# A chunked recurrence: the inverse's rows paced by the state's update, its operand fetched earlier, and half of the last norm's factors on ScalarE

## The chip, the cores and the metric

The kernel runs on one core of one Trainium2 chip. The metric is device time in microseconds (us), from the first to the last instruction with what lies around them; three runs stand behind the time before. The engines are TensorE (PE; PEld are its weight loads), VectorE (DVE), ScalarE (ACT), GpSimd (POOL) and SyncE (SP), whose queue issues nearly all DMAs.

## What is computed

A trunk of two layers on x of 2048 x 1024: first sliding-window attention, then RWKV-7 time mixing, each with a gated branch from per-layer inputs. The change touches the second layer's recurrence and the last RMS norm:

```python
def step(S, inp):                      # one token, 16 heads of 64 x 64 state
    sa = einsum('bhvk,bhk->bhv', S, -kk_t)
    S = S * d_t + sa[..., None] * (kk_t * a_t) + v_t[..., None] * k_t
    y = einsum('bhvk,bhk->bhv', S, r_t)
    return S, y
...
h = h + m
h = h + jax.nn.sigmoid(h @ ple_w_gate[i]) * (p[i] @ ple_w_proj[i])
return rms_norm(h, final_norm_g)
```

## The kernel before

Four phases follow each other: the attention's projections, the attention, the recurrence's projections and, from about 1950 us on, the recurrence (`rwkv`, L1176 on). The kernel computes the recurrence in 32 chunks of 64 tokens. Within a chunk the dependence of tokens on each other is a triangular system, whose inverse is needed for each of 16 heads; between chunks the state S is carried.

**Steps.** All work is written as Python generators, and `tick` (L574) advances each of the live ones by one `yield`. One tick is a step. `Dense.run` (L143) writes one step's worth of a dense product in each: three matmuls of 128x512 (L587 to L589, high and low parts of the operands), with the fetches, splits and evacuations around them. The recurrence's `chain(c)` (L1353) writes the chunk itself and puts steps between its parts: r1p (L1359) and 4 steps; y, up (L1371, L1379) and 5 steps; sp (L1386), the state's update and 9 steps. The update is st = sp + S on VectorE (L1388), two products uv = st x decay for the two halves (L1391), and S = st x decay on GpSimd (L1392). The next chunk's r1p reads uv. So a chunk has 18 steps, and a group of four chunks 72; in the text below, steps of a group are counted from 0, and its last chunk begins at step 54. Ahead of its steps a chunk writes its loads: `uv_tile(c + 1)`, bvt and szt (`load_bz`, L1405), x and xa of chunk c + 2 (`load_front`, L1229 to L1236). The former chunk's output is scaled in step 4 of a chunk and stored (gated, L1450).

**The inverse.** `tri(g)` (L1272) makes the inverses of four chunks at once, during the four chunks before them; `tris` (L1334) starts it when the first of these begins. Its operand ag (one buffer) comes by `load_ab` (L1340). Four transpositions (L1280), one per step, bring ag into P; GpSimd masks P (L1282); after three empty steps 30 rows follow, each a product into tmp (L1291) and a sum into P (L1293), of up to 240 elements per partition:

```python
for r in range(30, 0, -1):
    ...
    for _ in range(2 if r % 2 and 6 < r < 26 else 1):
        yield
```

Then come eight transpositions into at and tt (L1301, L1304), a copy on ScalarE (L1307), and twice, for two chunks each, products with ag (L1316), copies, four empty steps, products with tt (L1323) and copies. After the second half and one more step, `load_ab(g + 1)` is written. Counted so, the rows stand in steps 7 to 46 of a group, the second half's L1316 in step 61, its L1323 in step 65, and the load in step 66.

**The last norm.** `add_gate1` (L401) takes one of four column blocks n of 512 tokens: after its last tile, rs is made (L435 to L437, the power on GpSimd), and in eight further steps each of eight tiles res of 128x512 is multiplied by it (L442: k = 1 and 5 on GpSimd, the other six on VectorE) and stored (L443).

**Order.** The program is built with `schedule_with_timeline_sim=True` (L1503): the framework builds each engine's queue itself from the instructions as written and their dependences. Each queue then runs in its order on the chip, and an instruction at its head that has to wait holds those behind it.

Of the kernel before, what the change touches and what calls it, by code (L numbers as in the profile page):

```python
# [11 lines left out]
AF = mybir.ActivationFunctionType  # L12
ALU = mybir.AluOpType
# [7 lines left out]
NG = T // G  # L21
# [31 lines left out]
class Dense:  # L53
# [347 lines left out]
    def add_gate1(self, kind):  # L401

        tr, nc, ins = self.tr, self.nc, self.tr.ins
        NB = G // 128
        own, hs, sums = [], {}, {}

        def evac(n, ct, ps, hl, aux):
            th = self.tmp("th")
            self.gated(th, ps, hl, aux, (n, ct) == (NG - 1, KT - 1))
            if not own:  # L410
                own.append(self.cp.tile([128, C], F32, name="gnb"))
                nc.sync.dma_start(out=own[0], in_=ins["final_norm_g"].rearrange("(o c) -> o c", o=1).broadcast_to([128, C]))
            if ct == 0:
                sums[n] = self.cp.tile([128, NB, KT], F32, name="ss", bufs=2)
            ss = sums[n]
            for _ in range(9):
                yield
            for b in range(NB):
                nc.tensor.transpose(ps[:, b * 128:b * 128 + 128], th[:, b * 128:b * 128 + 128], tr.ident)
            res = hs[ct] = self.tmp("res", tag="h")  # L420
            blocks = lambda t: t.rearrange("p (b c) -> p b c", c=128)
            g = own[0][:, ct * 128:ct * 128 + 128].rearrange("p (o c) -> p o c", o=1).broadcast_to([128, NB, 128])
            last = (n, ct) == (NG - 1, KT - 1)
            if not last:
                nc.vector.tensor_tensor(out=blocks(res), in0=blocks(ps), in1=g, op=ALU.mult)
            for b in range(NB):
                sl = slice(b * 128, b * 128 + 128)
                nc.scalar.activation(th[:, sl], ps[:, sl], AF.Square, accum_out=ss[:, b, ct:ct + 1])
            if last:
                nc.vector.tensor_tensor(out=blocks(res), in0=blocks(ps), in1=g, op=ALU.mult)  # L430
            if ct < KT - 1:
                return
            yield
            rs = self.cp.tile([128, NB], F32, name="rs", bufs=2)
            nc.vector.tensor_reduce(out=rs, in_=ss, axis=mybir.AxisListType.X, op=ALU.add)  # L435
            nc.vector.tensor_scalar(out=rs, in0=rs, scalar1=1.0 / C, scalar2=1e-6, op0=ALU.mult, op1=ALU.add)
            nc.gpsimd.tensor_tensor(out=rs, in0=rs, in1=tr.mhalf.broadcast_to([128, NB]), op=ALU.pow)  # L437
            f = rs.rearrange("p (b o) -> p b o", o=1).broadcast_to([128, NB, 128])
            for k in range(KT):
                yield  # L440
                e = nc.gpsimd if k % 4 == 1 else nc.vector
                e.tensor_tensor(out=blocks(hs[k]), in0=blocks(hs[k]), in1=f, op=ALU.mult)  # L442
                nc.sync.dma_start(out=tr.out[n * G:n * G + G, k * 128:k * 128 + 128].rearrange("(b p) c -> p b c", p=128),  # L443
                                  in_=blocks(hs[k]))

        self.add(kind, w=ins["ple_w_gate"][1], fill=self.fill_direct, aux=self.load(tr.dram("ple1", [C, T])),
                 evac=evac, after="o")


class Trunk:  # L450
# [725 lines left out]
    def rwkv(self):  # L1176
        nc, ins = self.nc, self.ins
        LC = 64
        NP = KT
        NCH = T // LC  # L1180
        TG = 4
# [4 lines left out]
        with ExitStack() as es:  # L1186
# [85 lines left out]
            def tri(g):  # L1272


                ag = AG.pop(g)
                P = sm.tile([128, 32, 32], F32, name="P")
                PT = P.rearrange("u s t -> u t s")
                ga = ag.rearrange("q p c t -> q t (p c)")
                for i in range(0, 32, 8):
                    nc.vector.transpose(PT[:, i:i + 8], ga[:, i:i + 8])  # L1280
                    yield
                nc.gpsimd.affine_select(out=P, in_=P, pattern=[[-1, 32], [1, 32]], compare_op=ALU.is_gt, fill=0.0, base=0,  # L1282
                                        channel_multiplier=0)
                nc.gpsimd.memset(P.rearrange("u s t -> u (s t)")[:, 0:1024:33], 1.0)
                tmp = sm.tile([128, 240], F32, name="tmp")
                for _ in range(3):
                    yield
                for r in range(30, 0, -1):
                    n = 31 - r
                    t = tmp[:, 0:r * n].rearrange("u (s t) -> u s t", t=n)  # L1290
                    nc.vector.tensor_tensor(out=t, in0=P[:, 0:r, r:r + 1].broadcast_to([128, r, n]),  # L1291
                                            in1=P[:, r:r + 1, r + 1:].broadcast_to([128, r, n]), op=ALU.mult)
                    nc.vector.tensor_tensor(out=P[:, 0:r, r + 1:], in0=P[:, 0:r, r + 1:], in1=t, op=ALU.add)  # L1293
                    for _ in range(2 if r % 2 and 6 < r < 26 else 1):
                        yield
                tt = tts[g % 2]
                tv = tt.rearrange("q p c t -> q t (p c)")
                at = sm.tile([128, NP, TG, 32], F32, name="at")
                av = at.rearrange("q p c s -> q s (p c)")
                for i in range(0, 32, 8):  # L1300
                    nc.vector.transpose(av[:, i:i + 8], P[:, i:i + 8])  # L1301
                    yield
                for i in range(0, 32, 8):
                    nc.vector.transpose(tv[:, 32 + i:40 + i], PT[:, i:i + 8])  # L1304
                    yield
                for e in range(2):
                    nc.scalar.copy(tt[64 * e:64 * e + 32, :, :, 0:32], tt[64 * e:64 * e + 32, :, :, 32:64])  # L1307
                yield
                for j in range(0, TG, 2):


                    wt = sm.tile([128, 2, NP, 32], F32, name="wt")
                    wq = p_f.tile([128, 2, NP, 32], F32, name="wq", tag="f")
                    ops = [(i, p, 64 * e) for i in range(2) for p in range(NP) for e in range(2)]
                    for i, p, r0 in ops:
                        nc.tensor.matmul(wq[r0 + 32:r0 + 64, i, p], lhsT=ag[r0:r0 + 32, p, j + i, 32:64], rhs=at[r0:r0 + 32, p, j + i],  # L1316
                                         start=True, stop=True)
                    for e in range(2):
                        nc.scalar.copy(wt[64 * e + 32:64 * e + 64], wq[64 * e + 32:64 * e + 64])
                    for _ in range(4):  # L1320
                        yield
                    for i, p, r0 in ops:
                        nc.tensor.matmul(wq[r0:r0 + 32, i, p], lhsT=wt[r0 + 32:r0 + 64, i, p], rhs=tt[r0 + 32:r0 + 64, p, j + i, 32:64],  # L1323
                                         start=True, stop=True)
                    for e in range(2):
                        nc.scalar.copy(tt[64 * e:64 * e + 32, :, j:j + 2, 32:64],
                                       wq[64 * e:64 * e + 32].rearrange("q i p t -> q p i t"))
                    for i in range(2):
                        TT[g * TG + j + i] = tt[:, :, j + i]
                    yield  # L1330
                if (g + 1) * TG < NCH:
                    load_ab(g + 1)

            def tris():  # L1334
                for g in range(NCH // TG):
                    while chunk[0] < (g - 1) * TG:
                        yield
                    yield from tri(g)

            def load_ab(g):  # L1340
                AG[g] = sm.tile([128, NP, TG, LC], F32, name="ag")
                nc.sync.dma_start(out=AG[g].rearrange("q p c t -> q p (c t)"),
                                  in_=ab[:, g * TG * LC:(g + 1) * TG * LC].rearrange("(p q) t -> q p t", q=128))
# [9 lines left out]
            def chain(c):  # L1353
# [41 lines left out]
                if c + 2 < NCH:  # L1395
                    FR[c + 2] = front(c + 2)
                    next(FR[c + 2])
                self.start(output(c, y))
                self.ticks(STEPS[2])

            def load_bz(c):
                BZ[c] = tuple(r2.tile([128, NP, LC], F32, name=nm) for nm in ("bvt", "szt"))
# [47 lines left out]
                    nc.sync.dma_start(out=a, in_=yc[h])  # L1450
                self.outputs = c + 1

            chunk = [-TG]
            load_front(0)
            load_ab(0)
            self.start(tris())
            self.start(front(0))
            load_front(1)
# [48 lines left out]
```

## Time and profile before

| what | before |
|---|---|
| runs, median of 3 | 3054.29 us (3051.96 to 3057.05) |
| profiled execution, its own time | 3048.61 us |
| its span | 3046.4 us |
| mean granted clock of TensorE | 0.964 |
| PE busy | 2824.4 us (93%) |
| DVE busy | 1842.1 us (60%) |
| ACT busy | 1377.2 us (45%) |
| POOL busy | 962.2 us (32%) |

Times of single instructions and waits come from the one profiled execution, in us from the start of its span. A row of the timeline gives start, duration, engine, line, operation, the tile written and the tiles read, with shapes and count; in brackets stands how long the engine was idle before, and what ended that. Rows of PE overlap, as matmuls are pipelined.

### The profile page before, as it was taken

The numbers are of one execution on the slowest core, as the hardware profiler recorded it, in microseconds if no ns is written. First come the engines' busy times: TensorE is split into PE (matmuls) and PEld (weight loads), VectorE is DVE, ScalarE is ACT, GpSimd is POOL, SyncE is SP. The second block draws the span as 40 slices with busy tenths as digits, with TensorE's granted clock in tenths as the row PEclk, the third lists the DMA queues.
The fourth block names the chain that finished last, engine by engine and source line by source line (L and its number), as shares of the span: only waits on it lengthen the run. The fifth ranks groups of instructions, "written<-read, shape, count | busy, mean of one in ns | idle before, by whom it ended". The sixth has DMA issues, their size and how long they took to land. (4 is left out here: it accounts for less than half of the span.)

```text
span 3046.4 us, 56649 instructions
## 1 busy us (share of the span) xinstructions
PE 2824.4 (93%) x21416; PEld 2245.0 (74%) x21416; DVE 1842.1 (60%) x3489; ACT 1377.2 (45%) x2920; POOL 962.2 (32%) x850
## 2 busy tenths in 40 slices
PE   7999999999999999899999899989889879879987
PEld 5888887777777777587777678767767667667866
DVE  6532434776677655736777876685664774763444
ACT  5311114784465543525777843445434433334422
POOL 2242510001211242303666610224434435325421
PEclk9999999999999999999999999999999989889999
DMA  7664856999887587636656788989778779569674
GB/s 222 192 141 104 165 150 216 295 284 338 267 258 216 200 276 247 179 127 179 189 197 206 220 220 219 269 274 237 206 187 242 218 200 261 152 173 247 181 252 159
DMA packets 625233, 652.43 MB, mean 214 GB/s; under 512 B 261697, under 2 KB 435905, under 8 KB 624961
## 3 DMA queue, kind: packets, MB, share of 16 engines
q1 hardware_dynamic: 617280, 638.32, 70.6%
q0 software_dynamic: 7680, 10.50, 3.2%
q8 instruction: 169, 2.77, 0.4%
q14 instruction: 104, 0.84, 0.1%
HBM read 421.40 MB, written 216.79 MB: 209 GB/s over the span
## 5 line engine op out<-in xcount | busy, mean ns | idle before, releaser
L587 PE MATMUL ps<-dhi,dwh 128*128 128x512 f32 x1472 | 607.7, 414 | 25.2 <-ACT dwh L536 9.2
L589 PE MATMUL ps<-dhi,dwl 128*128 128x512 f32 x1472 | 591.0, 402 | 11.1 <-DVE dwl L538 6.8
L588 PE MATMUL ps<-dlo,dwh 128*128 128x512 f32 x1472 | 591.4, 403 | 4.9 <-POOL dlo L538 3.2
L587 PE MATMUL ps<-xH,wh 128*128 128x512 f32 x1408 | 553.4, 399 | 15.2 <-ACT xH L536 9.9
L588 PE MATMUL ps<-xL,wh 128*128 128x512 f32 x1408 | 558.7, 397 | 6.9 <-DVE xL L538 4.5
L589 PE MATMUL ps<-xH,wl 128*128 128x512 f32 x1408 | 558.2, 397 | 6.0 <-DVE wl L538 6.0
L587 PEld LDWEIGHTS ps<-dhi,dwh 128*128 128x128 f32 x1472 | 281.5, 191 | 96.5 <-ACT dwh L536 9.6
L589 PEld LDWEIGHTS ps<-dhi,dwl 128*128 128x128 f32 x1472 | 282.6, 192 | 77.0 <-DVE dwl L538 8.3
L588 PEld LDWEIGHTS ps<-dlo,dwh 128*128 128x128 f32 x1472 | 282.2, 192 | 63.1 <-POOL dlo L538 5.1
L587 PEld LDWEIGHTS ps<-xH,wh 128*128 128x128 f32 x1408 | 266.7, 191 | 78.7 <-ACT xH L536 14.5
L588 PEld LDWEIGHTS ps<-xL,wh 128*128 128x128 f32 x1408 | 268.2, 190 | 69.5 <-DVE xL L538 7.5
L589 PEld LDWEIGHTS ps<-xH,wl 128*128 128x128 f32 x1408 | 268.1, 190 | 65.2 <-DVE wl L538 8.4
L697 POOL DMA_DIRECT2D t<-t x160 | 126.1, 1250 | 201.2 <-issue 88.0
L871 ACT ACTIVATE S<-S,nm 128x256 f32<-128x256 f32 (+1 forms) x256 | 125.5, 492 | 69.2 <-DVE nm L868 62.1
L538 POOL TENSOR_TENSOR xL<-xs,xH 128x512 fp32r<-128x512 f32 x72 | 103.3, 1440 | 109.5 <-ACT xH L536 108.6
L536 ACT ACTIVATE wh<-wr 128x1024 fp32r<-128x1024 f32 x44 | 46.6, 1060 | 181.4 <-DMA wr<-in_attn_w_in 147.7
L862 DVE CUSTOM_DVE_ANT_0 S<-sc,mask,sink 128x256 f32<-128x256 f32 (+1 forms) x256 | 108.9, 471 | 22.1 <-PE sc L858 21.9
L1249 PE MATMUL aps<-xa,x 64*128 64x128 f32 x1024 | 99.7, 312 | 13.7 <-ACT bn L1268 5.6
L264 DVE TENSOR_TENSOR aux<-ps,aux 128x512 f32<-128x512 f32 x64 | 43.9, 686 | 109.7 <-PE ps L589 101.3
L1062 POOL TENSOR_TENSOR kb<-kb,mhalf 128x16 f32<-128x16 f32 x32 | 103.3, 3229 | 12.7 <-DVE kb L1061 12.2
L973 DVE SCALAR_TENSOR_TENSOR xs<-hp,mu,xs 128x512 f32<-128x512 f32 x96 | 80.8, 850 | 43.3 <-ACT xs L972 43.1
L1291 DVE TENSOR_TENSOR tmp<-P 128x30 f32<-128x30 f32 (+14 forms) x240 | 99.8, 416 | 11.2 <-POOL P L1282 4.5
(257 smaller groups left out, 5173.1 us busy)
## 6 DMA issues: line engine op xcount, KB each, us to landing
hp<-hn SPq DMA_DIRECT2D x72, 256.5 KB, 3.9
sz<-th SPq DMA_DIRECT2D x64, 256.0 KB, 4.6
ple<-pt SPq DMA_DIRECT2D x64, 256.0 KB, 6.4
aux<-ple SPq DMA_DIRECT2D x64, 256.0 KB, 4.6
yd<-kx SPq DMA_DIRECT2D x32, 512.0 KB, 4.3
dwh<-wp_ao SPq DMA_DIRECT2D x24, 512.0 KB, 5.5
dwl<-wp_ao SPq DMA_DIRECT2D x24, 512.0 KB, 6.4
dwh<-wp_ag SPq DMA_DIRECT2D x24, 512.0 KB, 4.4
```

Source lines behind the costliest of these rows:

```text
L536: nc.scalar.activation(hi, src, AF.Copy)
L538: e.tensor_tensor(out=lo, in0=src, in1=f32(hi), op=ALU.subtract)
L587: mm(ps, lhsT=wh, rhs=ah, start=first, stop=False)
L588: mm(ps, lhsT=wh, rhs=al, start=False, stop=False)
L589: mm(ps, lhsT=wl, rhs=ah, start=False, stop=last)
L697: nc.gpsimd.dma_start(out=t1[32 * d:32 * d + 32, :], in_=t2[32 * a:32 * a + 32, :], accum_op=ALU.add)
L862: nc.vector.tensor_tensor_reduce(out=S[:, i, c0:], in0=sc[:, eo, c0:], in1=mask[:, c0:], scale=1.0, scalar=sink[:, 4 * g + 2 * j + eo:4 * ...
L871: nc.scalar.activation(S[:, i, c0:], S[:, i, c0:], AF.Exp, bias=nm[:, i:i + 1], accum_out=den[:, i:i + 1])
L973: nc.vector.scalar_tensor_tensor(out=src, in0=t[:, :G], scalar=mus[:, c, k:k + 1], in1=src, op0=ALU.mult, op1=ALU.add)
L1062: nc.gpsimd.tensor_tensor(out=bs[:, :, 0], in0=bs[:, :, 0], in1=self.mhalf.broadcast_to([128, m]), op=ALU.pow)
L1249: nc.tensor.matmul(pse[eo][:, j], lhsT=x1[half[eo], 4 * i + j], rhs=xa[half[eo], 4 * i + j], start=True, stop=True)
L1291: nc.vector.tensor_tensor(out=t, in0=P[:, 0:r, r:r + 1].broadcast_to([128, r, n]), in1=P[:, r:r + 1, r + 1:].broadcast_to([128, r, n]), op ...
```

## The change

In the last norm, for n = 0, 1, 2, the tiles of odd k are multiplied on ScalarE, in four pieces of 128 columns with rs as scale; the last block stays as it was. In `tri` most single `yield`s become `yield from pause()`, which takes two steps if the second falls into the nine steps behind the state's update and else one; of the transpositions, two go with each pause; the rows' own doubling goes. `load_ab(g + 1)` moves in front of the four empty steps of the second half. After each inverse, six empty steps follow.

```diff
             for k in range(KT):
                 yield
-                e = nc.gpsimd if k % 4 == 1 else nc.vector
-                e.tensor_tensor(out=blocks(hs[k]), in0=blocks(hs[k]), in1=f, op=ALU.mult)
+                if k % 2 and n < NG - 1:
+                    for b in range(NB):
+                        nc.scalar.activation(hs[k][:, b * 128:b * 128 + 128], hs[k][:, b * 128:b * 128 + 128], AF.Copy,
+                                             scale=rs[:, b:b + 1])
+                else:
+                    e = nc.gpsimd if k % 4 == 1 else nc.vector
+                    e.tensor_tensor(out=blocks(hs[k]), in0=blocks(hs[k]), in1=f, op=ALU.mult)
...
                 for i in range(0, 32, 8):
                     nc.vector.transpose(PT[:, i:i + 8], ga[:, i:i + 8])
-                    yield
+                    if i % 16:
+                        yield from pause()
...
                     nc.vector.tensor_tensor(out=P[:, 0:r, r + 1:], in0=P[:, 0:r, r + 1:], in1=t, op=ALU.add)
-                    for _ in range(2 if r % 2 and 6 < r < 26 else 1):
-                        yield
+                    yield from pause()
...
                         nc.scalar.copy(wt[64 * e + 32:64 * e + 64], wq[64 * e + 32:64 * e + 64])
+                    if j + 2 == TG and (g + 1) * TG < NCH:
+                        load_ab(g + 1)
                     for _ in range(4):
                         yield
...
-                if (g + 1) * TG < NCH:
-                    load_ab(g + 1)
+
+            def pause():
+
+                yield
+                if update[0]:
+                    yield
...
                     yield from tri(g)
+                    for _ in range(6):
+                        yield
...
                 self.start(output(c, y))
+                update[0] = True
                 self.ticks(STEPS[2])
+                update[0] = False
...
-            chunk = [-TG]
+            chunk, update = [-TG], [False]
```

The transpositions into at and tt change as those of P do.

## Rows read from the trace of the kernel before

**Rows 1.** The page, section 4: the chain that ended last.
```profile
PE ps L587 6%; PE ps L589 5%; PE ps L588 5%; DVE tmp L1291 2%; DVE P L1293 2%; PE aps L1249 2%; DMA ag<-ab 1%; DMA raw<-gated 1%; PE sp L1386 1%; PE r1p L1359 1%; PE tp L1267 1%; PE y L1394 1%; PE up L1379 1%; PE wq L1316 1%; DVE uv L1391 1%
```

**Rows 2.** Busy time by chunk: PE, PEld, DVE, ACT, POOL, then clock, DMA share, GB/s.
```profile
2226.20:2257.50 31.30, 22.09 (x288) 17.91 (x287) 29.60 (x63) 8.59 (x15) 8.57 (x9) 0.91 0.58 164
2257.50:2286.40 28.90, 26.04 (x288) 21.36 (x288) 14.43 (x31) 9.87 (x16) 10.95 (x9) 0.87 0.79 196
2286.40:2307.20 20.80, 20.80 (x283) 16.93 (x282) 6.93 (x8) 11.75 (x20) 13.94 (x12) 1.00 0.98 249
```

**Rows 3.** PE's waits, 2110 to 2750 us: total, times, longest.
```profile
PE ps L419 <- DVE th L325: 21.0, 3, 8.9
PE r1p L1359 <- DVE uv L1391: 15.0, 3, 9.2
```

**Rows 4.** Timeline of DVE in chunk 8, the third group's first.
```profile
2226.15 2.37 DVE L1280 STREAM_TRANSPOSE P<-ag 128x256 f32<-128x256 f32 x4 [5.89 <-DMA ag<-ab]
...
2254.61 0.33 DVE L1291 TENSOR_TENSOR tmp<-P 128x168 f32<-128x168 f32 x1
2254.86 0.68 DVE L1388 TENSOR_TENSOR st<-sp,S 128x512 f32<-128x512 f32 x1
```

**Rows 5.** Timeline of PE: sp of chunk 8, and r1p behind three updates.
```profile
2239.05 1.15 PE L1386 MATMUL sp<-uv,bn 128*64 128x64 f32 x32
...
2257.50 2.49 PE L1359 MATMUL r1p<-uv,am 128*64 128x64 f32 x32 [9.21 <-DVE uv L1391]
...
2550.51 1.15 PE L1359 MATMUL r1p<-uv,am 128*64 128x64 f32 x32
...
2771.10 1.15 PE L1359 MATMUL r1p<-uv,am 128*64 128x64 f32 x32
```

**Rows 6.** DVE's waits, 2110 to 2750 us: total, times, longest.
```profile
DVE P L1280 <- DMA ag<-ab: 37.8, 6, 12.3
```

**Rows 7.** Groups of instructions, 2110 to 2740 us: the rows' two lines.
```profile
L1291 DVE TENSOR_TENSOR tmp<-P 128x30 f32<-128x30 f32 (+9 forms) x180 | 78.3, 435 | 9.4 <-POOL P L1282 4.5
L1293 DVE TENSOR_TENSOR P<-P,tmp 128x30 f32<-128x30 f32 (+9 forms) x179 | 73.9, 413 | 4.7
```

**Rows 8.** Timeline of SP's queue ahead of the last fetch of ag.
```profile
2680.31 2.81 SPq L1236 DMA_DIRECT2D xa<-rd  x1
2683.22 2.59 SPq L1405 DMA_DIRECT2D bvt<-bv  x2
2685.91 2.51 SPq L1405 DMA_DIRECT2D szt<-sz  x2
2688.46 1.65 SPq L1450 DMA_DIRECT2D gated<-yc  x2
2690.21 0.58 SPq L1342 DMA_DIRECT2D ag<-ab  x1
```

**Rows 9.** Timeline of PE: ag's last readers ahead of that fetch.
```profile
2684.48 1.20 PE L1316 MATMUL wq<-at,ag 32*32 32x32 f32 x64
```

**Rows 10.** Timeline of DVE: the norm's factors for n = 2.
```profile
2920.42 6.66 DVE L442 TENSOR_TENSOR res<-res,rs 128x512 f32<-128x512 f32 x5 [1.12 <-POOL rs L437]
...
2927.13 0.68 DVE L442 TENSOR_TENSOR res<-res,rs 128x512 f32<-128x512 f32 x1
2927.74 1.21 DVE L538 TENSOR_TENSOR dwl<-wraw,dwh 128x1024 fp32r<-128x1024 f32 x1
```

**Rows 11.** Timeline of PE: behind a short wait, and behind the wait for dwl.
```profile
2163.99 0.71 PE L1249 MATMUL aps<-xa,x 64*128 64x128 f32 x8 [2.04 <-ACT bn L1268]
...
2929.00 0.79 PE L589 MATMUL ps<-dhi,dwl 128*128 128x512 f32 x1 [6.04 <-DVE dwl L538]
...
2930.02 0.63 PE L588 MATMUL ps<-dlo,dwh 128*128 128x512 f32 x1
...
2934.53 0.39 PE L588 MATMUL ps<-dlo,dwh 128*128 128x512 f32 x1
```

**Rows 12.** Groups of instructions, 2900 to 2922 us: ScalarE's pieces of 128x128.
```profile
L428 ACT ACTIVATE th<-ps 128x128 f32<-128x128 f32 x12 | 3.1, 278 | 0.0
```

More of the change, by code (lines that the diff above doesn't have):

```diff
@@ L1301, in tri @@
                     nc.vector.transpose(av[:, i:i + 8], P[:, i:i + 8])
-                    yield
+                    if i % 16:
+                        yield from pause()
                 for i in range(0, 32, 8):
                     nc.vector.transpose(tv[:, 32 + i:40 + i], PT[:, i:i + 8])
-                    yield
+                    if i % 16:
+                        yield from pause()
                 for e in range(2):
```

## Prediction

> **What bounds the kernel now.** I began with the page: TensorE (PE) is busy nearly all the time, yet PE work is only a quarter of the chain that ended last, while the inverse's two lines on VectorE (L1291, L1293) and the fetch of its operand, ag, are named in it [rows 1]. So I looked for the places where PE stands. The table by chunk of the recurrence shows them: a chunk with no inverse beside it takes 20.8 us at a granted clock of 1.00, the first chunk of a group takes 31.3 and the second 28.9, at 0.91 and 0.87, with hardly more PE instructions [rows 2]. The list of waits from 2110 to 2750 us names what ended PE's idle time: a factor of the gate (th L325) and the state's update (uv L1391), both on VectorE [rows 3].
>
> VectorE's own timeline, first chunk of the third group, says why. The inverse's transpositions start at 2226.15, after 5.89 us of waiting for ag. Then its rows run back to back, and the update's sum (st) gets its turn at 2254.86 [rows 4], though PE had given its input, sp, at 2239.05 plus 1.15 [rows 5]: 14.7 us late. PE works off its steps and then waits 9.21 us for uv [rows 5]. Six groups do this (transpositions at 2119, 2226, 2344, 2455, 2584 and 2698); VectorE waits 37.8 us for ag in them [rows 6].
>
> One more thing is read there: **a queue's order is not the order written.** By the text two rows of the inverse stand ahead of the first chunk's st (steps 7 and 8 of the group; the update begins at step 9). In the queue 23 rows were done and the next begun (sizes up to 240 and down again to 168) [rows 4], and 18 to 27 over the six. What is ready goes first, some twenty steps ahead of its place, and the written place decides only between things that are ready together.
>
> **The change, part by part.**
>
> *The pace.* Counted in steps, the old text writes the 30 rows into steps 7 to 46 of a group of 72, the new one into 5 to 44: one per step in nine steps of a chunk, one per two steps in the other nine. "Half pace" is therefore no slower over the group; four rows instead of two are written ahead of the first update, all else moves by 0 to 3 steps. It removes no instruction. As the queue takes rows some twenty steps early, I cost it at 0. The bounds: two rows more in front of each of six updates, 2 x (0.435 + 0.413) [rows 7] x 6 = 10 us lost; or two fewer, 10 us gained. Zero, because both texts put every later row behind st, and the queue ignored that already [rows 4]. The six empty steps after an inverse fill time in which the generator waited for its chunk anyway: 0.
>
> *The fetch.* load_ab moves from behind the second half's products to behind the last readers of ag (L1316), five written steps sooner. It is one DMA on SP's queue. What does it pass there? SP's order before ag is the same in five of six groups: x, xa, bvt, szt, gated, ag [rows 8]. x and xa are written later than ag and went ahead since they were ready earlier; bvt, szt and gated are written at steps 54 to 58 of the group, ahead of ag's old step 66 and of its new step 60. Nothing in this row of transfers is written between the two places. The last readers ran at 2684.48 and end 1.2 us later [rows 9]; ag is issued at 2690.21, when SP has done what lies before it: SP's backlog holds it for 4.5 us here. So I cost the move at 0 (two raw loads of the group at 2119 might be passed, 1 us). Bounds: nothing lost, as a fetch can't be issued before its buffer is free in either text; above, all of VectorE's 37.8 us of waiting [rows 6]. I take the lower end: SP's queue is nearer to the question than the wait that it causes.
>
> *Half of the last norm's factors.* For n = 0, 1 and 2, VectorE loses two of its six products of 128x512, GpSimd its two, and ScalarE gets 4 x 4 of 128x128. The number of output DMAs stays. For n = 0 and 1 (2540 and 2762 us) the next r1p, at 2550.51 and 2771.10, had no wait [rows 5], so 0: nine steps of PE work cover it, and without them it would be a few us of ScalarE. For n = 2 it matters: the products stand ahead of dwl, a weight's low part, and PE waits 6.04 us for that [rows 10, 11]. From the first product to dwl are 2927.74 - 2920.42 = 7.3 us; five products took 6.66, or 1.33 each, while GpSimd worked beside them, and the last, alone, 0.68 [rows 10]. Four remain: between 4 x 0.68 = 2.7 and 4 x 1.33 = 5.3. GpSimd keeps two subtractions there, so two at either price: 4.0. That is 7.3 - 4.0 = 3.3 us sooner, and PE waits 2.7.
>
> The Trainium skill (SBUF — State Buffer, "SBUF: two separate sides") says that VectorE with two SBUF inputs and GpSimd reading SBUF hold one port pair by turns, so that one blocks the other fully. By it alone, with GpSimd's products gone, four products at 0.68 would save 4.6 us; by the row's mean, 2.0. The trace agrees with the rule (1.33 against 0.68), and my 3.3 lies between.
>
> After the wait of 6.04 PE's products take 0.63 us each until 2933.86, and 0.39 at 2934.53 [rows 11]: the two levels of its clock. They come 0.43 us apart and then 0.235, so 11 of them cost 11 x 0.19 = 2.1 us. After a wait of 2.04 us at 2163.99, eight small products took 0.71 us, the quick pace [rows 11]. A wait of 2.7 is nearer to that: I take the 2.1 too. ScalarE pays 16 x 0.278 = 4.4 us [rows 12] while PE waits; if the factors stood ahead of ScalarE's copies of the accumulators, PE's next one would be late by up to 4.4 us, and SP would wait for ScalarE's tiles with the next weights' loads behind. Bounds of this part: 8.1 gained (the whole wait and the slow stretch), 2 lost (4.4 less the 2.7 that PE waits anyway).
>
> *Sum.* 0 + 0 - 3.3 - 2.1 = -5.4. The profiled execution took 3048.61 us (span 3046.4), so 3043.2 there. It is 5.7 below the median of the runs, 3054.29; against that median the forecast is **3048.9**. About 0.2% (6.1 us) is what a measurement of this kernel tells from no change, so this stands just inside it. What is late next: the state's update behind the rows, as before.
>
> **The rivals.**
> 1. *The fetch comes early after all.* If the queue takes ag ahead of bvt, szt and gated, VectorE's waiting goes and the rows run while PE has work. For it: 37.8 us of waiting, and 36 us of PE's waits behind it [rows 3, 6]. Against: SP's order. Between half and all of the 37.8, say 28: 3054.3 - 5.4 - 28 = 3020.9.
> 2. *The update falls further back (slower).* L1316 is written a step sooner (18 steps in 20.8 us, 1.2 us each [rows 2]), so the queues place the inverse a step sooner against PE's work, while on the chip ag is held by SP's backlog as before. VectorE then has 1.2 us more of rows, and the two written ahead (1.7 us), in front of st: 2.9 x 6 = 17.4, less 5.4: 3066.3. It decides from the point at which first chunks show more than 27 rows ahead of st.
> 3. *Nothing moves.* The queue puts dwl elsewhere, or ScalarE's factors hold PE's accumulators, and the 5.4 is not had: 3054.3.
>
> **How the numbers follow.** Forecast 0.42 (its own range 3046 to 3056, from the bounds of the last part), rival 1 0.20, rival 2 0.22, rival 3 0.16. Half of the forecast's cases lie a little over 6.1 us below: with rival 1, faster by over 0.2% is 0.41; slower 0.22; the rest, 0.37, within. The range is 3020 to 3067: it leaves out rival 1's deeper half and the far end of rival 2.
>
> **What would show it.** Right: SP's order x, xa, bvt, szt, gated, ag unchanged, VectorE waiting for ag some 30 to 40 us over six groups, st of first chunks 7 to 15 us behind sp, and at 2925 us a wait of PE for dwl of 2 to 3 us with four products ahead of it. Wrong: ag issued within 2 us of its last reader, and first chunks of 22 to 25 us (rival 1); or first chunks longer than 31 us with more rows ahead of st (rival 2). The queues are rebuilt as a whole, so single waits elsewhere may come and go by some us; were they to sum to more than 6, the forecast would fail for a reason that these rows can't show.

## The result, and the profile after

| | median, us | runs |
|---|---|---|
| before | 3055.99 | 11 |
| changed | 3070.37 | 11 |

The ratio is 1.0051, with a 95% interval of 1.0036 to 1.0066: the change costs 14.4 us. The profiled execution of the changed kernel took 3078.18 us (span 3076.4), and that of before 3048.61. These two lie 29.6 us apart, twice the 14.4 of the medians: the rows below show where time goes, and the sizes are taken from the runs.

Lines have moved: the inverse's first transpositions are L1285 now (L1280 before), its rows L1297 and L1299 (L1291, L1293), st L1403, uv L1406, r1p L1374, sp L1401, ag's fetch L1357, the last norm's factors on VectorE L447.

Where the time went is read from the third group again. Busy time by chunk, chunks 7 to 10 of the changed kernel (columns as in [rows 2]):

```profile
2204.04:2240.15 36.11, 28.49 (x543) 23.32 (x543) 15.09 (x19) 19.50 (x35) 14.83 (x12) 0.91 0.80 218
2240.15:2278.49 38.34, 25.11 (x287) 20.37 (x287) 33.49 (x79) 9.76 (x16) 9.43 (x10) 0.81 0.39 110
2278.49:2304.14 25.65, 24.83 (x286) 20.25 (x287) 9.68 (x14) 7.89 (x14) 11.60 (x10) 0.88 0.89 221
2304.14:2324.96 20.82, 20.82 (x282) 16.94 (x281) 7.60 (x8) 11.75 (x20) 13.22 (x12) 1.00 1.00 253
```

And chunk 7 of the kernel before, which the rows ahead of the prediction don't have:

```profile
2196.45:2226.20 29.75, 27.57 (x543) 22.29 (x542) 14.93 (x18) 19.02 (x34) 15.97 (x12) 1.00 0.92 230
```

The last chunk of the group before takes 6.4 us more (36.11 for 29.75), the group's first chunk 7.0 more (38.34 for 31.30 in [rows 2]); the two behind it give 3.2 back. So two places cost, one of them **ahead** of the group (with the pace alone, the first experiment below, chunks 7 and 8 take 35.5 and 38.4 us). VectorE's timeline over both:

```profile
2218.20 2.37 DVE L543 TENSOR_TENSOR dlo<-xs,dhi 128x512 fp32r<-128x512 f32 x2
2235.67 2.27 DVE L1285 STREAM_TRANSPOSE P<-ag 128x256 f32<-128x256 f32 x4 [15.11 <-DMA ag<-ab]
2237.85 0.65 DVE L1403 TENSOR_TENSOR st<-sp,S 128x512 f32<-128x512 f32 x1
2238.53 2.75 DVE L1406 TENSOR_TENSOR uv<-st,decay 64x512 f32<-64x512 f32 x2
...
2271.18 2.26 DVE L1310 STREAM_TRANSPOSE tt<-P 128x256 f32<-128x256 f32 x4
2276.22 0.69 DVE L303 SCALAR_TENSOR_TENSOR th<-th,ps 128x512 f32<-128x512 f32 x1 [2.78 <-ACT th L302]
2276.83 0.68 DVE L1403 TENSOR_TENSOR st<-sp,S 128x512 f32<-128x512 f32 x1
```

and PE's rows for the same updates:

```profile
2222.99 1.15 PE L1401 MATMUL sp<-uv,bn 128*64 128x64 f32 x32
2240.15 0.44 PE L1374 MATMUL r1p<-uv,am 128*64 128x64 f32 x2 [6.15 <-DVE uv L1406]
...
2256.75 1.15 PE L1401 MATMUL sp<-uv,bn 128*64 128x64 f32 x32
2278.49 0.45 PE L1374 MATMUL r1p<-uv,am 128*64 128x64 f32 x2 [12.49 <-DVE uv L1406]
```

Two readings. In chunk 7 the transpositions stand in front of st, where before they stood behind it and uv. VectorE waits 15.11 us for ag with st queued behind that wait: st's input was there at 2222.99 + 1.15, st begins 13.7 us later, and PE waits 6.15. (VectorE's queue is served strictly in order: the Trainium skill, PSUM — Partial Sum Buffer, "Engine vs sequencer instructions", says so, and this row agrees.) In chunk 8 all 30 rows of the inverse, and even its last transpositions (tt, L1310), stand ahead of st (23.5 rows before): st is 18.9 us behind sp (14.7 in [rows 4, 5]), and PE waits 12.49 us (9.21 in [rows 5]).

Counted in VectorE's queue, the rows ahead of the first st of groups two to seven:

| group | 2 | 3 | 4 | 5 | 6 | 7 |
|---|---|---|---|---|---|---|
| before | 18 | 23.5 | 18 | 20.5 | 24 | 27.5 |
| changed | 18.5 | 30 | 17.5 | 28 | 23.5 | 20.5 |
| transpositions ahead of the uv before | no | yes | no | yes | no | yes |

(The last line is the changed kernel's; before, it is so in the seventh group alone, where they stand between st and uv.)

The loss sits in two groups: chunks 7 to 10 take 120.9 us (110.7 before) and chunks 15 to 18 137.8 (125.8). These are the third and fifth group, which have both the transpositions ahead and the most rows. The seventh has the transpositions ahead too, but fewer rows than before, and loses nothing: chunks 23 to 27 take 153.7 us, 154.2 before.

In the fifth group one transposition stands ahead of st and three between st and uv; VectorE, then PE:

```profile
2477.79 0.73 DVE L1285 STREAM_TRANSPOSE P<-ag 128x256 f32<-128x256 f32 x1 [21.44 <-DMA ag<-ab]
2478.39 0.65 DVE L1403 TENSOR_TENSOR st<-sp,S 128x512 f32<-128x512 f32 x1
```

```profile
2492.53 1.09 PE L419 MATMUL ps<-ident,th 128*128 128x128 f32 x4 [10.46 <-DVE th L325]
2493.55 1.98 PE L1374 MATMUL r1p<-uv,am 128*64 128x64 f32 x32
```

and PE of the kernel before:

```profile
2456.16 0.45 PE L1359 MATMUL r1p<-uv,am 128*64 128x64 f32 x6
2465.52 1.09 PE L419 MATMUL ps<-ident,th 128*128 128x128 f32 x4 [8.92 <-DVE th L325]
2466.54 1.76 PE L1359 MATMUL r1p<-uv,am 128*64 128x64 f32 x26
```

Counted to the first product of the next r1p, chunk 15 takes 47.4 us here (2446.12 to 2493.55) and took 31.4 before. Most of that difference is only where the mark falls: PE's queue has the reader of the gate's factor th (L419) ahead of r1p here, and had it behind the first 6 of r1p's 32 products before. The other 26 ran at 2466.54, 41.8 us into chunk 15. So some 5.6 us are lost, and the gate's wait (10.46 and 8.92 us) is in both. Waits over six groups, 2110 to 2790 us, to be held against [rows 6] and [rows 3]:

```profile
DVE P L1285 <- DMA ag<-ab: 65.3, 5, 21.4
```

```profile
PE r1p L1374 <- DVE uv L1406: 32.2, 10, 12.5
PE ps L419 <- DVE th L325: 18.8, 3, 10.5
```

SP's queue ahead of ag's fetch, third group, has the order of [rows 8] still:

```profile
2218.56 2.37 SPq L1241 DMA_DIRECT2D xa<-rd  x1
2221.02 1.74 SPq L1422 DMA_DIRECT2D bvt<-bv  x2
2222.85 1.98 SPq L1422 DMA_DIRECT2D szt<-sz  x2
2224.88 2.41 SPq L1467 DMA_DIRECT2D gated<-yc  x2
2227.39 0.57 SPq L1357 DMA_DIRECT2D ag<-ab  x1
```

The end of the kernel answers [rows 10] on VectorE and [rows 11] on PE:

```profile
2952.72 4.39 DVE L447 TENSOR_TENSOR res<-res,rs 128x512 f32<-128x512 f32 x4 [1.12 <-POOL rs L437]
2957.16 1.21 DVE L543 TENSOR_TENSOR dwl<-wraw,dwh 128x1024 fp32r<-128x1024 f32 x1
```

```profile
2958.43 0.80 PE L594 MATMUL ps<-dhi,dwl 128*128 128x512 f32 x1 [3.41 <-DVE dwl L543]
2959.45 0.63 PE L593 MATMUL ps<-dlo,dwh 128*128 128x512 f32 x1
...
2963.72 0.48 PE L593 MATMUL ps<-dlo,dwh 128*128 128x512 f32 x1
2964.04 0.40 PE L594 MATMUL ps<-dhi,dwl 128*128 128x512 f32 x1
```

Four products in place of six, the wait for dwl down from 6.04 to 3.41 us, and the matmuls behind it again at 0.63 us each for some 4.7 us.

### The profile page after: what moved, and what is told of

It reads as the page before. It is cut to its first block, busy times and chain, and to the rows that moved or that the text cites. A ratio compares the mean times of both kernels' runs of the same rounds, so it can differ in the third digit from the quotient of the medians.

```text
span 3076.4 us, 56683 instructions
## 1 busy us (share of the span) xinstructions
PE 2833.3 (92%) x21416; PEld 2249.2 (73%) x21416; DVE 1840.9 (60%) x3483; ACT 1391.4 (45%) x2968; POOL 949.2 (31%) x844
## 5 line engine op out<-in xcount | busy, mean ns | idle before, releaser
L592 PE MATMUL ps<-xH,wh 128*128 128x512 f32 x1408 | 552.2, 398 | 14.4 <-ACT xH L541 7.8
L1297 DVE TENSOR_TENSOR tmp<-P 128x30 f32<-128x30 f32 (+14 forms) x240 | 103.1, 430 | 10.7 <-POOL P L1288 4.1
```

Of the source, the lines that this page charges most:

```text
L592: mm(ps, lhsT=wh, rhs=ah, start=first, stop=False)
```

## The experiments

Every ratio below is against the kernel before, run beside it on the same chip (its medians: 3052.4 to 3054.2 us).

**The parts alone.** The kernel before with the pace's edits only, and with ScalarE's factors only.

```diff
# pace_alone
+                    if i % 16:
+                        yield from pause()
...
+                    yield from pause()
...
+                    for _ in range(6):
+                        yield
# factors_alone
+                if k % 2 and n < NG - 1:
+                    for b in range(NB):
+                        nc.scalar.activation(hs[k][:, b * 128:b * 128 + 128], hs[k][:, b * 128:b * 128 + 128], AF.Copy,
+                                             scale=rs[:, b:b + 1])
```

> The kernel before with the pace alone (pairs of transpositions in one step, one row per step or per two steps, six empty steps after each inverse); the load and the factors as before. In its VectorE queue the transpositions of the third, fifth and seventh inverse stand ahead of the st of the chunk before, as in the changed kernel, and 30 and 28 rows ahead of the first st of the third and fifth group. Theory 1 (these places cost the time: VectorE stands for ag with st queued behind it): 14 to 20 us slower than before, so at the changed kernel's time or up to 5 us above it, and 55 to 75 us of waiting for ag over the six groups (37.8 before). Theory 2 (the moved load or ScalarE's factors cost the time): within 5 us of before.

> The kernel before with the factors alone (ScalarE applies half of them). Theory 1, with the prediction's term for this part: 2 to 6 us faster than before, the wait of PE for dwl near 2925 us down from 6.0 to some 3 us. Theory 2 (ScalarE's factors hold back its copies for PE): 5 to 15 us slower than before.

Measured: pace alone 3073.3 us, 1.0057 (1.0036 to 1.0077); factors alone 3051.7, 0.9997 (0.9985 to 1.0010). The pace is the whole loss: 0.57% or 17 us, as Theory 1 expected, with 69.8 us of waiting for ag over the six groups. The factors gain 0.9 us by the ratio, 4.6 at most, where 2 to 6 were expected; they don't cost anything. The load's move was not run alone: neither in the kernel before nor beside the pace does it change any instruction's place in any of the five queues.

**A step more.** The changed kernel with 1, and with 6, empty steps ahead of the first transposition, from the third inverse on.

```diff
+                for _ in range(1 if g > 1 else 0):      # 6 in six_steps_later
+                    yield
                 ag = AG.pop(g)
```

> The changed kernel with one empty step ahead of the first transposition from the third inverse on, nothing else. In the VectorE queue every inverse's transpositions then stand behind the st of the chunk before, and 17 to 27.5 rows ahead of the first st of a group. Theory 1: the loss goes; 12 to 20 us faster than the changed kernel, so within 6 us of before on either side. Theory 3 (the pace as such, rows spread differently over a group, is what costs, wherever they start): within 4 us of the changed kernel, some 14 us slower than before.

> The changed kernel with six empty steps ahead of the first transposition from the third inverse on. In the VectorE queue 18, 12.5, 9.5, 7 and 7.5 rows then stand ahead of the first st of groups three to seven (23.5, 18, 20.5, 24 and 27.5 before). Theory 1, carried on: the st of first chunks comes 5 to 14 us sooner in five groups and ag has landed when it is asked for: 10 to 40 us faster than before. Theory 4 (the inverse is itself late for the next group when it starts later, so that PE waits for tt in place of uv): no faster than with one step, or slower.

Measured: 3047.1, 0.9983 (0.9970 to 0.9996), and 3026.9, 0.9911 (0.9893 to 0.9928). One empty step undoes the loss and a little more; the pace as such (Theory 3) doesn't cost it. Six steps beat both kernels by 27 and 43 us, though VectorE waits 48.0 us for ag there. All these waits stand behind st and uv, and fewer rows stand ahead of the first st, so this run doesn't tell the two readings apart.

**The pair.** The kernel before with its first transpositions in pairs; the changed kernel with that pair undone.

```diff
                     nc.vector.transpose(PT[:, i:i + 8], ga[:, i:i + 8])
-                    yield
+                    if i % 16:
+                        yield from pause()
```

(In the first, where `pause` is one plain step; the second has the reverse.)

> The kernel before with one edit: the four first transpositions of an inverse in two steps in place of four (the row pace, the load and the factors as before). In its VectorE queue the transpositions of the third and sixth inverse stand ahead of the st of the chunk before; rows ahead of the first st are 24.5 and 24.5 there (23.5 and 24 before), 19.5, 16.5 and 18 in the fourth, fifth and seventh group (18, 20.5, 27.5 before). Theory 1a (the wait for ag ahead of that st is what costs): 10 to 13 us lost in the third and in the sixth group, a few us won in the seventh; 8 to 22 us slower than before. Theory 1b (only the count of rows ahead of the first st costs): 5 us slower to 8 us faster.

> The changed kernel with one edit undone: its four first transpositions take four steps again (two of them with a step between, as before). In VectorE's queue all transpositions stand behind the uv of the chunk before, and 18, 16.5, 18, 14.5, 16 and 15 rows ahead of the first st of groups two to seven (18, 23.5, 18, 20.5, 24, 27.5 before). If place and rows are what counts: 15 to 30 us faster than the changed kernel, 2 to 14 us faster than before. If the loss has another source in the change: within 5 us of the changed kernel.

Measured: 3047.4, 0.9975 (0.9966 to 0.9985), and 3042.9, 0.9957 (0.9942 to 0.9973). The second says that without the pair the change would have been a gain of 0.4%, 10 to 13 us: it is the edit on which the loss hangs. The first was a miss for Theory 1a: 7 us faster where it expected 8 to 22 slower. Theory 1b's range (5 slower to 8 faster) holds it. Its transpositions do stand ahead of st twice; the third and sixth group's:

```profile
2225.28 2.35 DVE L1280 STREAM_TRANSPOSE P<-ag 128x256 f32<-128x256 f32 x4 [7.23 <-DMA ag<-ab]
...
2588.45 2.27 DVE L1280 STREAM_TRANSPOSE P<-ag 128x256 f32<-128x256 f32 x4 [26.58 <-DMA ag<-ab]
```

The third costs little, since ag was issued at 2219.38, 17.6 us into chunk 7 (23.4 in the changed kernel), and chunk 7 takes 2.7 us more than before, chunk 8 4.9 less. The sixth costs 6.4 us in chunk 19. Against that the seventh group's first st has 18 rows ahead of it in place of 27.5: chunk 24 is 10.6 us shorter, chunk 25 6.8 longer. So transpositions ahead of st cost time in one group and not in the other; in the changed kernel the two groups that lose have 30 and 28 rows as well.

**Who issues ag.** ag's DMA on ScalarE, behind the copies that wait for its last readers, in the changed kernel, the kernel before and the one with six steps.

```diff
-                nc.sync.dma_start(out=AG[g].rearrange("q p c t -> q p (c t)"),
+                nc.scalar.dma_start(out=AG[g].rearrange("q p c t -> q p (c t)"),
```

> The changed kernel with ag's DMA issued by ScalarE, where it stands right behind the copies that wait for ag's last readers, in place of SP, where x, xa, bvt, szt and gated stand ahead of it. VectorE's queue keeps the transpositions ahead of st and 30 and 28 rows ahead of the first st. Theory 1a: ag comes 4 to 5 us sooner in each of six groups, the waits for it fall from 65 to under 40 us, and the kernel is 15 to 30 us faster than the changed one (5 to 15 faster than before). Theory 1b: the rows still stand ahead of st, at most 10 us faster than the changed one, still slower than before.

> The kernel before with ag's DMA issued by ScalarE; the queues of PE, VectorE and GpSimd are those of before, instruction for instruction. If SP's backlog is what makes ag late (the prediction's first rival): ag is issued some 4.5 us sooner in each of six groups, VectorE's waiting for it falls from 37.8 to some 10 us, and the kernel is 8 to 27 us faster. If ag's issue was not late by the backlog, or ScalarE's issue costs as much as it brings: within 5 us of before.

> The changed kernel with six empty steps ahead of the first transposition from the third inverse on, and ag's DMA issued by ScalarE. The kernel with the six steps alone still waits 48 us for ag. If these waits stand on the path to the st of first chunks: 10 to 25 us faster than the six steps alone (3002 to 3017 us). If the rows have time to spare there by now: within 5 us of it.

Measured: 3064.5, 1.0032 (1.0017 to 1.0047); 3039.4, 0.9952 (0.9938 to 0.9967); 3031.8, 0.9925 (0.9912 to 0.9938). The kernel before gains 15 us by nothing but another issuer, and its waits for ag fall from 37.8 to 25.2 us. ScalarE in that run, seventh group:

```profile
2680.00 1.17 ACT L1319 COPY wt<-wq 32x512 f32<-32x512 f32 x2 [0.91 <-PE wq L1316]
2681.20 0.40 ACTq L1342 DMA_DIRECT2D ag<-ab  x1
```

The last readers (from 2678.70, 1.20 us) had ended at 2679.90: ag goes out 1.3 us behind them, not 4.5 [rows 8, 9]. What is left of the wait is the landing: its transpositions begin 8.5 us behind the issue (2689.66), 7.6 in the kernel before. The changed kernel gains 6 us only, with intervals that overlap, as Theory 1b had it. But it still waits 55.0 us for ag (under 40 expected), 20.0 of them in the fifth group, so the run hardly tests Theory 1a. The kernel with six steps gains nothing, where 10 to 25 us were expected. (The Trainium skill, DMA: Bandwidth & Descriptors, "Issuing engines are not separate DMA queues", says that a second issuer saves only the sequencer's time, usually small against the transfer. By its own time the issue is indeed small, 0.40 and 0.58 us; but moved out from behind the others on SP's queue, it made 15 us here.)

**The transpositions put back, the rows left.** First held behind the last st written ahead of them, then behind the last uv: an order on VectorE's queue, no wait.

```diff
-                    nc.vector.transpose(PT[:, i:i + 8], ga[:, i:i + 8])
+                    with behind():
+                        nc.vector.transpose(PT[:, i:i + 8], ga[:, i:i + 8])
...
+            def behind():
+                return self.tc.issue_after(ST[0].ins) if ST else ExitStack()
...
-                    nc.vector.tensor_tensor(out=t, in0=sp, in1=S, op=ALU.add)
+                    ST[0] = nc.vector.tensor_tensor(out=t, in0=sp, in1=S, op=ALU.add)
```

(In the second kernel `ST[0]` is set at the products uv instead.)

> The changed kernel with the first transpositions of every inverse held behind the last st written ahead of them in VectorE's queue (an order on one engine, no wait). The rows ahead of the first st of each group stay as in the changed kernel: 18.5, 30, 17.5, 28, 23.5 and 20.5. Theory 1a (the wait for ag ahead of the st of the chunk before costs): 10 to 17 us faster than the changed kernel, within 4 us of before. Theory 1b (the count of rows ahead of the first st costs): within 5 us of the changed kernel.

> The changed kernel with the first transpositions of each inverse held in VectorE's queue behind the last uv written ahead of them, not behind st alone (in the kernel with the hold behind st they came to stand between st and uv in three groups, so uv still waited for ag). Ahead of the first st of groups two to seven stand 18.5, 30, 17.5, 26, 29.5 and 22 rows, as many as in the changed kernel or more. Theory 1a (the wait for ag ahead of the uv of the chunk before costs): 8 to 17 us faster than the changed kernel, within 6 us of before. Theory 1b (the count of rows ahead of the first st costs): within 5 us of the changed kernel, or slower.

Measured: 3066.0, 1.0049 (1.0029 to 1.0069), and 3058.2, 1.0018 (1.0005 to 1.0030). The first looked like a verdict for the rows alone, and wasn't. Third group:

```profile
2226.91 0.69 DVE L1408 TENSOR_TENSOR st<-sp,S 128x512 f32<-128x512 f32 x1 [2.84 <-PE sp L1406]
2238.74 2.27 DVE L1287 STREAM_TRANSPOSE P<-ag 128x256 f32<-128x256 f32 x4 [11.14 <-DMA ag<-ab]
2240.92 2.30 DVE L1411 TENSOR_TENSOR uv<-st,decay 64x512 f32<-64x512 f32 x2
```

st was early, but PE reads uv, and the transpositions had slipped between the two. Behind uv, chunks 7 and 8 come apart:

```profile
2200.34:2229.33 28.99, 27.36 (x544) 22.16 (x543) 13.74 (x15) 18.92 (x34) 14.25 (x11) 1.00 0.90 236
2229.33:2268.15 38.82, 22.14 (x287) 17.89 (x287) 35.77 (x82) 8.39 (x13) 9.87 (x10) 0.84 0.45 127
```

Chunk 7 is back to 29 us, chunk 8 with its 30 rows ahead of st stays at 38.8. Chunk 15 still takes 44.8. In the whole, the hold behind uv takes back 0.33% of the 0.51%, some 10 us (4 to 16 by the two intervals). Not all of it is the place: the trace counts 26.5, 22 and 19.5 rows ahead of the first st of groups five to seven, not the 26, 29.5 and 22 expected. That is 4 rows fewer than in the changed kernel, some 3 us at the prediction's 0.85 us a row. The 0.18% that stay against before, some 5 us (2 to 9), are put down to the rows.

**VectorE's queue in the written order.** Transpositions (as above) and rows of the inverse held in that way, in both texts.

```diff
+                    with behind():
+                        nc.vector.tensor_tensor(out=t, in0=P[:, 0:r, r:r + 1].broadcast_to([128, r, n]),
+                                                in1=P[:, r:r + 1, r + 1:].broadcast_to([128, r, n]), op=ALU.mult)
+                        nc.vector.tensor_tensor(out=P[:, 0:r, r + 1:], in0=P[:, 0:r, r + 1:], in1=t, op=ALU.add)
```

> The changed kernel with transpositions and rows of the inverse held behind the last st written ahead of each, so that VectorE's queue follows the text: 4 rows ahead of the first st of a group, 13 in the second chunk, 13 in the third (before: 18 to 27.5, 12 to 2.5 and none). Theory 1b, and the prediction's reading of rows 4 and 5 (st is late because rows stand ahead of it): first chunks fall from 31 to 22 to 25 us, second ones from 29 to 22 to 26, third ones rise by 2 to 4; 25 to 60 us faster than before. If the inverse's end is then late for the products that wait for it, so that the next group starts late: no faster than before.

> The kernel before with the same hold: 2 rows ahead of the first st of a group, 13, 13 and 2 in the chunks behind it. If the pace as written makes no difference once the queue follows it (the prediction's cost of the pace, 0): within 6 us of the changed kernel held in the same way. If the later end of its rows (step 46 of 72) or the later load costs: 6 to 20 us slower than that.

> The changed kernel held in the written order, with ag's DMA issued by ScalarE. If ag's lateness still holds the four first rows and so st: 5 to 20 us faster than the written order alone. If st no longer hangs on ag (it stands behind four rows only when ag is in time): within 5 us of it.

> The changed kernel with transpositions and rows held behind the last uv written ahead of each. Against the hold behind st alone (3013.6 us) the transpositions no longer stand between st and uv in three groups. If that place cost the wait for ag and 2.4 us of transpositions there: 12 to 30 us faster than that, level with before in the written order (2984). If the pace itself costs (the pair and four rows ahead of the first st in place of four steps and two rows): within 6 us of 3013.6.

> The kernel before with the same hold behind uv. Only the seventh group had its transpositions between st and uv in the hold behind st (2983.9 us): 0 to 8 us faster than that. This and the run before it tell the price of the pace once the queue follows the text: equal within 6 us if it has none, 15 to 30 us apart if it has.

> The kernel before, held behind uv, with ag's DMA issued by ScalarE. VectorE waits 39.5 us for ag in the hold behind st. If the first rows, and with them the st behind them, still wait for ag: 5 to 20 us faster than without. If PE has other work by then: within 5 us.

| | held behind | us | ratio, interval |
|---|---|---|---|
| changed | st | 3013.6 | 0.9869 (0.9846 to 0.9891) |
| changed, ag from ScalarE | st | 3005.2 | 0.9839 (0.9816 to 0.9863) |
| changed | uv | 3001.6 | 0.9836 (0.9818 to 0.9854) |
| before | st | 2983.9 | 0.9775 (0.9753 to 0.9797) |
| before | uv | 2992.3 | 0.9805 (0.9785 to 0.9824) |
| before, ag from ScalarE | uv | 2986.1 | 0.9779 (0.9760 to 0.9799) |

This is the prediction's reading of [rows 4, 5] put to the test, and it holds: with two rows ahead of the first st, and 13, 13 and 2 in the chunks behind it, the kernel before is 69 us faster. The changed text with the same hold gains 39 (25 to 60 expected). Chunks 8 to 10 of the kernel before, held behind st:

```profile
2216.51:2238.51 22.00, 22.00 (x288) 17.86 (x287) 12.16 (x30) 8.59 (x15) 10.81 (x10) 1.00 0.85 238
2238.51:2260.73 22.22, 22.22 (x288) 18.07 (x287) 17.90 (x34) 7.89 (x14) 9.59 (x8) 1.00 0.95 216
2260.73:2282.27 21.54, 21.27 (x281) 16.78 (x280) 18.12 (x31) 11.75 (x20) 12.87 (x11) 1.00 0.99 252
```

31.3, 28.9 and 20.8 us [rows 2] have become 22.0, 22.2 and 21.5, all at a granted clock of 1.00, and st (2230.53) begins 0.04 us behind its sp (from 2229.34, 1.15 us):

```profile
2230.53 0.69 DVE L1394 TENSOR_TENSOR st<-sp,S 128x512 f32<-128x512 f32 x1 [1.13 <-PE sp L1392]
```

```profile
2229.34 1.15 PE L1392 MATMUL sp<-uv,bn 128*64 128x64 f32 x32
```

What the rows cost by themselves is the step from the transpositions behind uv (1.0018) to transpositions and rows behind uv (0.9836): the rows ahead of the six first st fall from 134 to 24 together, and 56 us go, some 0.5 us a row. At that price the changed kernel's 138 rows would cost 3 us against the 131.5 of before.

Between the two texts lie 29.7 us when held behind st (against "within 6 us", or the old one slower: a miss), 9.3 when held behind uv, with intervals that overlap. The changed text has its transpositions between st and uv in three groups in the first case, the old one in one. For the changed text, moving the hold behind uv saved 12 us (the lower end of what was expected); for the old one it cost 8, where 0 to 8 gained were expected. Both pairs of intervals overlap, so neither step is clear of noise. ag from ScalarE brings 6 to 8 us more (2992.3 to 2986.1, 3013.6 to 3005.2), again within overlapping intervals.

One difference of the two texts shows in the traces. In the changed text, held behind st, ScalarE's copy of the inverse (tt, L1317) stands right ahead of its copies uv (L1402) in four groups of six; in the old text in none. In the seventh group it waits there for the inverse's last transpositions, and PE's sp waits for uv behind it; ScalarE, then PE:

```profile
2743.41 2.10 ACT L1317 COPY tt<-tt 32x1024 f32<-32x1024 f32 x2 [8.85 <-DVE tt L1313]
2745.51 1.17 ACT L1402 COPY uv<-up 64x512 f32<-64x512 f32 x2
```

```profile
2746.74 1.98 PE L1407 MATMUL sp<-uv,bn 128*64 128x64 f32 x32 [6.54 <-ACT uv L1402]
```

From 2110 to 2790 us PE's sp waits 17.9 us for ScalarE's uv, and 18.9 with the hold behind uv; in the old text 2.3 and 1.0. That speaks for a cost of the pace's own once VectorE's queue is held: again an instruction with a wait ahead of the path's next operation, on another engine. How much of the 29.7 and 9.3 us it makes was not tested.

**The version to which this points**: before, held behind st, with ag and half of the last factors on ScalarE.

> The kernel before held behind st in the written order (2983.9 us), with ScalarE's half of the last factors and ag's DMA issued by ScalarE. ag from ScalarE brought 15 us to before and 6 us to the hold behind uv; the factors alone 1 us: 2970 to 2986 us, the fastest of all. If the one st of the seventh group that stands ahead of the transpositions, not its uv, sets the end: no faster than 2984.

Measured: 2980.9, 0.9761 (0.9741 to 0.9781): the lowest median of all, though its interval takes in the 0.9775 of the hold alone, so what ag and the factors add there is not clear of noise. It beats the kernel before by 72 us and the changed one by 89.

## Why the prediction was wrong

**What bounds the kernel**: right. The time hangs on when VectorE comes to the state's update; the held kernels show what it is worth.

**The pace, costed at 0**: the step that failed. "Zero, because both texts put every later row behind st, and the queue ignored that already": the queue ignores the written place, but it isn't blind to a step. The pace alone made +17 us, with the load and the factors as before. Two things lie in it. The prediction counted rows ("four rows instead of two are written ahead of the first update, all else moves by 0 to 3 steps") and did not follow the other operations that were moved, the transpositions, each of which carries the wait for ag. They seem to cost most: ahead of a uv for which PE is waiting, about 10 us, of which some 3 may be the rows'. And the rows ahead of the first st went to 30 and 28 in two groups: about 5 us as what is left, 3 by the price of a row. That the two together make the loss is shown by the runs that undo both (one step more, the pair undone); the split is an estimate. The bounds of ±10 us were taken from the rows alone and are too narrow for that reason.

**The six empty steps, 0**: right. They were not run by themselves, but without them no instruction of the changed kernel changes its place in any of the five queues.

**The fetch, 0**: right. ag still stands behind x, xa, bvt, szt and gated, and the load's move changes no place in any queue. SP's backlog as the cause of ag's lateness was right too: rival 1's price for an early fetch, 28 us, came out as 15 in the run that issued ag from ScalarE, since the landing stays.

**The factors, −5.4**: right in mechanism, too large. Four products took 4.39 us, not 4.0, and PE waited 3.41, not 2.7: 2.6 gained of the 3.3. The 2.1 of slow matmuls were not had: the row taken for the quick pace had a wait of 2.04 us in front, and behind 3.41 the matmuls ran at 0.63. Alone the part measured −0.9 us (−4.6 to +3.1), which leaves room for the 2.6 and not for 5.4.

**The rivals.** The second (the update falls back, 3066.3) came nearest, with its mark: more than 27 rows ahead of the first st, here in two groups. Its price of 17.4 for the pace met the 17 measured, but partly by luck: the rows didn't grow in all six groups, and by the estimate above the larger half came from the transpositions, which it doesn't mention. The range ended at 3067 because it left out "the far end of rival 2"; that is where the result lies. The sign of the forecast was wrong.

**What would show it**: SP's order held, as did the four products ahead of dwl. VectorE's waiting for ag (65.3, not 30 to 40 us) and st's lateness in the third group's first chunk (18.9 us, not 7 to 15) spoke against the forecast at once.

## What to carry to other kernels

Where a builder orders the queues, look first at which instructions carry a wait, and what the path needs that stands behind each of them; a step's difference in the text can put such an instruction ahead of the path's next operation. If an order on one engine decides the time, write it down as an order between instructions (here 69 us by holding two kinds of instruction behind a third) instead of tuning the step at which each is written. Hold behind the operation that the other engine reads: transpositions held behind st only, with uv left behind them, took nothing back (1.0049). And look at the other engines' queues too, as the copy tt ahead of uv on ScalarE shows.

## What the runs showed of the hardware

After its wait of 3.41 us PE's products came back at 0.63 us each, the lower of the clock's two levels: the granted clock is 0.50 from 2958.4 to 2963.7 us and 1.00 from 2964 to 2970. Around the wait of 2.04 us in [rows 11], from 2162 to 2166 us, it is 1.00. The chunks shown in which PE was busy throughout (20.80, 20.82, 22.00 and 22.22 us) ran at 1.00.

In the changed kernel one of the inverse's instructions, 128x84, took 0.23 us at 2243.06, while GpSimd stood idle (from 2240.82 to 2243.46), and the like of it 1.32 at 2267.35, beside one of GpSimd's sums of 128x512 (from 2267.30, 1.26 us):

```profile
2243.06 0.23 DVE L1299 TENSOR_TENSOR P<-P,tmp 128x84 f32<-128x84 f32 x1
...
2267.35 1.32 DVE L1299 TENSOR_TENSOR P<-P,tmp 128x84 f32<-128x84 f32 x1
```

Here the short instruction of VectorE took as long as the long one of GpSimd beside it.
